# Split GELU times gate on one core: the steps in which the first tile is computed

## The chip, the cores and the metric

The kernel runs on one core of a Trainium2 chip. The core has engines that work side by side: ScalarE (ACT) computes functions element by element, VectorE (DVE) multiplies and adds tensors, SyncE (SP) issues transfers, and sixteen DMA engines move data between the chip's main memory (HBM) and the on-chip memory (SBUF, 128 partitions). TensorE and GpSimd have no work here. The metric is the device time of one execution in microseconds (us). Before the change it is 469.36 us, the median of three runs from 469.31 to 469.44.

## The reference

```python
batch, seq, dim = (32, 512, 2048)
x = np.random.randn(batch, seq, dim).astype(np.float32)

half_dim = x.shape[-1] // 2
x1, x2 = (x[..., :half_dim].copy(), x[..., half_dim:].copy())
gelu_x1 = 0.5 * x1 * (1 + erf(x1 / np.sqrt(2)))
return (gelu_x1 * x2).astype(np.float32)
```

The input has 16,384 rows of 2,048 numbers, 134.2 MB. The first half of a row goes through GELU and is multiplied with the second half. The output has rows of 1,024 numbers, 67.1 MB.

## The kernel before, in words

The rows are cut into 16 tiles of 1,024 rows. In a tile each of the 128 partitions holds R = 8 rows next to each other, so that one partition's part of a load is one piece of 64 KB of HBM, and its part of a store one piece of 32 KB. There are two input buffers (`x0`, `x1`) and two output buffers (`o0`, `o1`), and tile i uses the buffers i % 2: even tiles share one pair and odd tiles the other.

Loads are issued on SP's queue (`load`, L49), q1 in the profile. Tile 0 is loaded in two halves of four rows per partition, each with a semaphore of its own (`first[0]`, `first[1]`), tile 1 in one piece; all three are issued ahead of the loop. Stores (`store`, L56) are issued on ACT's queue, q10 in the profile, but for the last two tiles, whose stores go on SP's queue. Tile 0 and tile 15 are stored in two halves of four rows per partition, all others in one piece.

In the loop each tile is computed in steps, runs of its eight rows. Every step is one ACTIVATE on ACT (GELU of the first half of the rows, from the input buffer into the output buffer, L87) and one multiply on DVE (output buffer times the second half of the rows, in place, L95), which waits for its ACTIVATE through `gelu_done`. Tiles 1 to 14 have steps of five and three rows; tiles 0 and 15 have steps of two, two and four (`steps` at L79). Shapes in the profile name the elements of one partition: 2, 3, 4, 5 rows are 128x2048, 128x3072, 128x4096, 128x5120.

What sets the order of the work is written out by hand:

- Each engine's queue runs in program order. On ACT a store's issue stands between the ACTIVATEs and waits there for `mul_done`, the count of multiplies that are done; whatever ACT has to do next stands behind it.
- For tile 0, the ACTIVATE of row 0 waits for `first[0]` and that of row 4 for `first[1]` (L82). For later tiles the first ACTIVATE waits for `ready[k]`, which counts both the tile's load and the last store out of the same output buffer. So a tile starts when its load has landed and the store of the tile two before it has too.
- After tile i, SP waits until its multiplies are done and issues the load of tile i + 2 (`if i + 2 < n_tiles` at the end of the loop).
- A transfer's rows (128, one for each partition) are spread over the sixteen DMA engines, eight for each, and followed on each engine by a small end marker that raises the semaphore.

```python
steps = ((0, 2), (2, 4), (4, 8)) if pieces else ((0, 5), (5, 8))
...
if pieces and hi % 4 == 0:
    if last:
        store(nc.sync, i, slice(hi - 4, hi), tail_stored)
    else:
        store(nc.scalar, i, slice(hi - 4, hi), ready[k])
```

Of the kernel before, what the change touches and what calls it, by code (L numbers as in the profile page):

```python
# [1 line left out]

# [4 lines left out]

GELU = mybir.ActivationFunctionType.Gelu


@with_exitstack
def kernel(
    ctx: ExitStack,
    tc: tile.TileContext,
    x: bass.AP,
    out: bass.AP,
):
    nc = tc.nc
    P = nc.NUM_PARTITIONS

    x_flat = x.flatten_outer_dims()
    out_flat = out.flatten_outer_dims()
    n_rows, dim = x_flat.shape
    half = dim // 2

    R = 8
    x_t = x_flat.rearrange("(n p r) d -> n p r d", p=P, r=R)
    o_t = out_flat.rearrange("(n p r) d -> n p r d", p=P, r=R)
    n_tiles = x_t.shape[0]
    x_bufs = [nc.alloc_sbuf_tensor(f"x{k}_tile", [P, R, dim], x.dtype) for k in range(2)]  # L30
    o_bufs = [nc.alloc_sbuf_tensor(f"o{k}_tile", [P, R, half], out.dtype) for k in range(2)]

    first = [nc.alloc_semaphore(f"first{j}") for j in range(2)]
    ready = [nc.alloc_semaphore(f"ready{k}") for k in range(2)]
    gelu_done = nc.alloc_semaphore("gelu_done")
    mul_done = nc.alloc_semaphore("mul_done")
    tail_stored = nc.alloc_semaphore("tail_stored")
    opened = nc.alloc_semaphore("opened")  # L40
    scrap = nc.alloc_sbuf_tensor("scrap_tile", [8, 128], x.dtype)
    n = {sem.name: 0 for sem in [*first, *ready, gelu_done, mul_done, tail_stored, opened]}

    def counted(ins, sem, by):
        ins.then_inc(sem, by)
        n[sem.name] += by

    def load(i, rows, sem):
        ins = nc.sync.dma_start(out=x_bufs[i % 2][:, rows, :], in_=x_t[i][:, rows, :])  # L49
        counted(ins, sem, 16)  # L50
        return ins

    def store(queue, i, rows, sem):
        queue.wait_ge(mul_done, n[mul_done.name])
        counted(
            queue.dma_start(out=o_t[i][:, rows, :], in_=o_bufs[i % 2][:, rows, :]), sem, 16  # L56
        )

    opening = nc.scalar.dma_start(out=scrap[:, :], in_=x_t[0][:8, 0, :128])
    counted(opening, opened, 16)
    for ins in (
        opening,
        load(0, slice(0, 4), first[0]),
        load(0, slice(4, 8), first[1]),
        load(1, slice(0, 8), ready[1]),
    ):  # L70
        tc.no_tile_sem_insts.add(ins.ins.name)
    tc.close()
    tc.compile()  # L73

    for i in range(n_tiles):
        k = i % 2
        last = i == n_tiles - 1
        pieces = i == 0 or last
        steps = ((0, 2), (2, 4), (4, 8)) if pieces else ((0, 5), (5, 8))  # L79
        for lo, hi in steps:  # L80
            rows = slice(lo, hi)
            if i == 0 and lo % 4 == 0:  # L82
                nc.scalar.wait_ge(first[lo // 4], 16)
            elif lo == 0:
                nc.scalar.wait_ge(ready[k], n[ready[k].name])
            counted(
                nc.scalar.activation(  # L87
                    out=o_bufs[k][:, rows, :], in_=x_bufs[k][:, rows, :half], func=GELU
                ),
                gelu_done,  # L90
                1,
            )
            nc.vector.wait_ge(gelu_done, n[gelu_done.name])
            counted(
                nc.vector.tensor_mul(  # L95
                    out=o_bufs[k][:, rows, :],
                    in0=o_bufs[k][:, rows, :],
                    in1=x_bufs[k][:, rows, half:],
                ),
                mul_done,  # L100
# [7 lines that stand above are left out]
        if not pieces:  # L108
            if i == n_tiles - 2:
                store(nc.sync, i, slice(0, R), tail_stored)  # L110
            else:
                store(nc.scalar, i, slice(0, R), ready[k])
        if i + 2 < n_tiles:
            nc.sync.wait_ge(mul_done, n[mul_done.name])
            load(i + 2, slice(0, R), ready[k])


    nc.scalar.wait_ge(opened, 16)
    nc.scalar.drain()  # L119
    for sem in (*first, *ready, opened):  # L120
        nc.scalar.sem_clear(sem)
    nc.vector.drain()
    nc.vector.sem_clear(gelu_done)
    nc.sync.sem_clear(mul_done)
    nc.sync.wait_ge(tail_stored, n[tail_stored.name]).then_inc(
        tail_stored, -n[tail_stored.name]
    )


# [1 line left out]
_INS = ['x']  # L131
_OUTS = [((32, 512, 1024), 'float32')]


# [23 lines left out]
```

## Time and profile before

| What | Value |
|---|---|
| Median of three runs | 469.36 us |
| Profiled execution, span from first to last instruction | 467.8 us |
| Median less span | 1.56 us |
| ACT busy | 115.5 us, 25% |
| DVE busy | 140.5 us, 30% |
| Moved by the DMA engines | 201.34 MB, mean 430 GB/s |
| Queue q1 (loads, last stores) | 142.61 MB, 70.6% of the engines' time |
| Queue q10 (the other stores) | 58.73 MB, 29.1% of the engines' time |

The profile is of one execution. It gives its span, and no other time of its own; the median of the runs stands 1.56 us above the span. Single instructions of tile 0 and of the last tile have these means: an ACTIVATE of 128x2048 takes 1,901 ns and one of 128x4096 3,608 ns; a multiply of 128x2048 takes 2,288 ns and one of 128x4096 4,424 ns.

The profile shows busy times of the engines, a row that gives the share of time in which the DMA engines were busy in each of 40 slices (9 is 90% or more), the packets of each DMA queue, and a chain of waits: the work that ended last, followed back step by step to what released it. A DMA packet of a load or store is one partition's piece, and "to landing" counts from a transfer's issue until its last end marker.

### The profile page before, as it was taken

The page shows a single profiled execution, that of the slowest core. Times are in us where ns is not written, and L with a number is a line of the kernel's source. Part 1 is how long each engine was busy: PE and PEld are TensorE (multiplying, and loading weights), DVE is VectorE, ACT ScalarE, POOL GpSimd, SP SyncE. Part 2 cuts the span into 40 slices and gives each one's busy share as a digit, 9 for nine tenths or more (in the row PEclk, how much of TensorE's full clock was granted, in tenths as well). Part 3 has the DMA queues.
Part 4 walks back from the last instruction along what each step waited for, and adds up shares of the span by engine and source line. Part 5 has one row for each costly group of instructions (what it writes and reads, how often), then busy time and mean ns, then how long its engine had stood idle before and what let it go on. Part 6 is the DMA issues. An engine that isn't in the chain of part 4 may idle for free.

```text
span 467.8 us, 154 instructions
## 1 busy us (share of the span) xinstructions
DVE 140.5 (30%) x34; ACT 115.5 (25%) x35; POOL 0.2 (0%) x4
## 2 busy tenths in 40 slices
DVE  0330515207051060511606115060150702507043
ACT  1320606041060410604105050050501506014060
POOL 0000000000000000000000000000000000000000
DMA  8999999999999999999999999999999999999988
GB/s 359 448 448 448 398 406 496 403 403 448 459 437 403 440 412 493 403 403 448 487 409 403 445 406 493 403 403 448 493 403 403 448 426 471 403 426 426 493 384 379
DMA packets 5057, 201.34 MB, mean 430 GB/s; under 512 B 568, under 2 KB 576, under 8 KB 576
## 3 DMA queue, kind: packets, MB, share of 16 engines
q1 hardware_dynamic: 2880, 142.61, 70.6%
q10 hardware_dynamic: 2176, 58.73, 29.1%
q14 instruction: 1, 0.01, 0.0%
HBM read 134.22 MB, written 67.11 MB: 430 GB/s over the span
## 4 chain that ended last, share of the span: by engine, by line
DMA 76%; DVE 14%; ACT 8%; ACTq 0%; SPq 0%; issue 0%
DMA out_dram<-o_tile 66%; DVE o_tile L95 14%; DMA x_tile<-in_x_dram 10%; ACT o_tile L87 8%; ACTq L119 0%; SPq L49 0%
## 5 line engine op out<-in xcount | busy, mean ns | idle before, releaser
L95 DVE TENSOR_TENSOR o_tile<-o_tile,x_tile 128x5120 f32<-128x5120 f32 (+3 forms) x34 | 140.5, 4171 | 319.7 <-ACT o_tile L87 319.7
L87 ACT ACTIVATE o_tile<-x_tile 128x5120 f32<-128x5120 f32 (+3 forms) x34 | 114.3, 3407 | 337.3 <-DMA out_dram<-o_tile 301.8
L87 ACT ACT_TABLE_LOAD x1 | 1.3, 1283 | 2.9 <-PEq L73 2.9
L142 POOL MEMSET const-bfloat16-1.0<- 128x1 bf16 x1 | 0.1, 102 | 0.0
L142 POOL MEMSET const-uint8-127<- 128x1 uint8 x1 | 0.1, 101 | 0.0
L142 POOL MEMSET const-float32-0.0<- 128x1 f32 x1 | 0.1, 99 | 0.2 <-issue 0.2
L142 POOL MEMSET const-float32-1.0<- 128x1 f32 x1 | 0.1, 98 | 0.0
## 6 DMA issues: line engine op xcount, KB each, us to landing
out_dram<-o_tile ACTq DMA_DIRECT2D x13, 4096.0 KB, 44.7
x_tile<-in_x_dram SPq DMA_DIRECT2D x2, 4096.0 KB, 16.7
out_dram<-o_tile ACTq DMA_DIRECT2D x2, 2048.0 KB, 34.4
out_dram<-o_tile SPq DMA_DIRECT2D x1, 4096.0 KB, 25.2
out_dram<-o_tile SPq DMA_DIRECT2D x2, 2048.0 KB, 7.8
x_tile<-in_x_dram SPq DMA_DIRECT2D x15, 44.4
scrap_tile<-in_x_dram ACTq DMA_DIRECT2D x1, 4.0 KB
```

Source lines behind the costliest of these rows:

```text
L87: nc.scalar.activation(out=o_bufs[k][:, rows, :], in_=x_bufs[k][:, rows, :half], func=GELU),
L95: nc.vector.tensor_mul(out=o_bufs[k][:, rows, :], in0=o_bufs[k][:, rows, :], in1=x_bufs[k][:, rows, half:],),
L142: nc = _bacc.Bacc("TRN2", target_bir_lowering=False, num_devices=1)
```

## The change

Tile 0 is computed in two steps of four rows each, where it had steps of two, two and four. The loads of tile 0 (two halves) and its stores (two halves of four rows, issued after the multiplies of rows 3 and 7) are the same, and so is every other tile.

```diff
         pieces = i == 0 or last
-        steps = ((0, 2), (2, 4), (4, 8)) if pieces else ((0, 5), (5, 8))
+        if i == 0:
+            steps = ((0, 4), (4, 8))
+        else:
+            steps = ((0, 2), (2, 4), (4, 8)) if last else ((0, 5), (5, 8))
         for lo, hi in steps:
```

On ACT and on DVE two instructions of 128x2048 become one of 128x4096, so that each of the two engines has one instruction less. In the changed file the lines behind the edit stand three lower: L87 becomes L90 and L95 becomes L98.

## The prediction

> **What bounds the kernel now.** I read the page first: ACT is busy 25% and DVE 30% of the span, while the DMA line stands at 9 in nearly every slice.
>
> ```profile
> DVE 140.5 (30%) x34; ACT 115.5 (25%) x35; POOL 0.2 (0%) x4
> ...
> DMA  8999999999999999999999999999999999999988
> ...
> HBM read 134.22 MB, written 67.11 MB: 430 GB/s over the span
> ```
>
> So the sixteen DMA engines are the bound; DVE and ACT together could rest half the time. The size of one transfer unit comes next. A load or store of 128 partitions is 128 rows, 8 for each DMA engine. Tile 0's second load lands 9.68 us after the first (22.45 against 12.77), so a row of 32 KB takes 1.21 us, one of 64 KB (a whole load) 2.42, one of 16 KB (half a store) 0.61. A tile is then 8 x 2.42 + 8 x 1.21 = 29.04 us, and 16 tiles 464.6 us of the 467.8. The rest is 1.7 us before the first row, 0.45 after the last, and about 1 us of small gaps and stretched rows. Nothing that happens on ACT or DVE can save more than this 1 us; it can only add idle time on the DMA engines.
>
> The chain of waits (start, length, what) seems to say something else, and shows where an edit could still matter:
>
> ```profile
> 1.64 45.36 DMA x_tile<-in_x_dram
> 46.99 0.02 issue
> 47.02 4.48 ACT o_tile L87
> ...
> 60.31 40.07 DMA out_dram<-o_tile
> 100.38 0.02 issue
> 100.40 4.48 ACT o_tile L87
> ...
> 403.75 44.74 DMA out_dram<-o_tile
> 448.49 0.02 issue
> 448.51 1.91 ACT o_tile L87
> ```
>
> It runs through the odd tiles: 1, 3, ... 15, each 58.0 us after the last. While an odd tile is computed, the DMA engines work off an even tile's rows (2 x 29.04 = 58.1), so the 13 us of ACT and DVE in each round are covered. Tile 0 is not in this chain at all. It touches it only through the order in which its stores' rows stand among the loads' rows.
>
> **Tile 0, step by step.** The timeline of before (start, length, instruction) gives the start; the durations of a step of four rows are already in the trace, from tile 0's second half and the last tile:
>
> ```profile
> 12.79 3.71 ACT L87 ACTIVATE o_tile<-x_tile 128x2048 f32<-128x2048 f32 x2 [8.65 <-DMA x_tile<-in_x_dram]
> 14.73 4.49 DVE L95 TENSOR_TENSOR o_tile<-o_tile,x_tile 128x2048 f32<-128x2048 f32 x2 [14.73 <-ACT o_tile L87]
> 19.26 0.38 ACTq L56 DMA_DIRECT2D out_dram<-o_tile  x1
> 22.47 3.62 ACT L87 ACTIVATE o_tile<-x_tile 128x4096 f32<-128x4096 f32 x1 [5.97 <-DMA x_tile<-in_x_dram]
> 26.12 4.42 DVE L95 TENSOR_TENSOR o_tile<-o_tile,x_tile 128x4096 f32<-128x4096 f32 x1 [6.89 <-ACT o_tile L87]
> 30.58 0.36 ACTq L56 DMA_DIRECT2D out_dram<-o_tile  x1
> ```
>
> Removed: two ACTIVATEs and two multiplies of 2048 elements (3.71 and 4.49 us). Added: one of each of 4096 (3.62 and 4.42). Busy time falls by 0.1 us on each engine, worth nothing beside an idle engine. What moves is the overlap: DVE began at 14.73, after half of ACT's work; now it begins after all of it, at 12.79 + 3.62 + 0.03 = 16.44, and ends at 20.86. The first store of tile 0 (call it A) is issued at **20.90 instead of 19.26, 1.64 us later**. Behind it on ACT's queue stands the GELU of rows 4 to 8, which waits for its load until 22.45; A's issue is over at 20.90 + 0.38 = 21.28, so 1.17 us of cover are left. From 22.47 on tile 0 is as before: the second store (B) and the load of tile 2 are issued at 30.58 and 30.57, with tile 1's load far from done (46.99). No other instruction moves on SP, ACT or DVE by itself.
>
> **What 1.64 us do to A's rows.** This is the first thing that the trace of before does not show directly. The DMA view by stretches shows how the two queues (q1: loads, q10: stores) take turns on every engine:
>
> ```profile
> q1 hardware_dynamic: 32, 1.05, 99.0%
> ...
> q10 hardware_dynamic: 16, 0.26, 152.8%
> ...
> q1 hardware_dynamic: 16, 1.05, 93.6%
> ...
> q10 hardware_dynamic: 16, 0.26, 122.2%
> ```
>
> These are the packets that start in 21.6 to 24.3 us, 24.3 to 24.7, 24.7 to 27.3 and 27.3 to 27.8. In the first, sixteen load rows of 64 KB (and tile 0's sixteen end markers); then sixteen store rows, sixteen load rows, sixteen store rows: one row of each queue in turn. A, issued at 19.26, got no turn at 21.66 to 22.11, where tile 1's first row started, but the one after it, at 24.36. An engine with nothing before it was quicker: the first load, issued at 0.73, had all its first rows under way between 1.73 and 2.30, that is 1.00 to 1.57 us after the issue. So A could have run from 20.3 to 20.8 on, and yet the next row, 0.8 to 1.9 us later, was another's: the choice is made ahead, by at least about 1.3 us on each engine, perhaps when the row before it starts.
>
> After the change A is there at 21.9 to 22.5, and the turn at 24.1 to 24.7 is about 2.2 us away. If the choice is made over 2.2 us ahead (one row of 64 KB is 2.42 us), A misses this turn and its first row starts near 26.8; if it is made 1.3 to 2.2 us ahead, nothing changes at all. I take the miss, because a choice at the start of a row of 2.42 us fits both, and one engine of sixteen that misses is enough.
>
> [...]
>
> **What a missed turn costs.** The rows of A, then B, then every later store stand one load row further back. Tile 1 gains: the eighth row of A is no longer ahead of its end marker, so it starts 0.61 us earlier, at 46.4. From tile 2 on each tile waits for the store before last in its output buffer, whose end now stands behind the next load's first row: starts move by 2.42 us (71.40 to 73.8, 100.40 to 102.8, and so on). That is no idle time: loads and stores are issued some 14 us before the queues ahead of them are empty (load 4 at 84.69, load 3 done at about 99), so the engines never starve, and the lag does not grow.
>
> It shows at the end. Behind store 13 stands no load any more but store 14 on q1, a row of 1.21 us: tile 15 starts at 448.51 + 1.21 = 449.72, and its last store is issued 1.21 us later. In before:
>
> ```profile
> 454.97 5.57 SPq L56 DMA_DIRECT2D out_dram<-o_tile  x2
> 455.76 4.42 DVE L95 TENSOR_TENSOR o_tile<-o_tile,x_tile 128x4096 f32<-128x4096 f32 x1 [0.81 <-ACT o_tile L87]
> ```
>
> The second of these issues starts at 454.97 + 5.57 - 0.33 = 460.21 and its rows from 462.07 on, without a gap behind the store before it. So 1.86 us lie between them, and an issue needs 1.00 to 1.57 (the first load, above): 0.29 to 0.86 us of cover. The loss is 1.21 less this: **0.35 to 0.92 us**, middle 0.64. The store before it (454.97, first row at 457.2) has 2.23 us between, and its loss of at most 0.55 lies inside the later one.
>
> [...]
>
> **The sum.** Span 467.8 + 0.64 = 468.4; the median of the runs, 469.36, lies 1.56 us above the profiled span, which I keep: **470.0 us**. About 0.2%, or 0.94 us, is what a measurement of this kernel can tell from no change, so the forecast itself is "no change", a little on the slow side.
>
> **The rivals.**
> 1. No missed turn: A takes its row at 24.36 as before. Everything after it stands where it stood: 469.36. For it: the lead that before proves is only 1.3 us. Against it: a choice at row starts explains before as well.
> 2. Slower: a missed turn with nothing to hide it at the end. If an issue from SP needs all of the 1.86 us, the whole 1.21 is lost: 470.57; and if the engines run dry they start again with a stretched row, as the first did (1.64 to 2.06 instead of 1.21: 0.43 to 0.85 more), up to 471.4. It decides from an issue-to-row time above 1.59 us (1.21 - 0.94 = 0.27 of cover left). For it: before needs A to be not yet chosen 1.2 to 1.6 us after its issue. Against: no row shows such a time on an engine that was free.
> 3. Faster: the chain of waits taken at its word. Tile 1 starts 0.61 us earlier and all odd tiles with it, 468.75. Against it: the bytes. 464.6 us of rows leave about 1 us in the whole span to save, and stores that come late push odd tiles too. Even so it ends 0.61 below, inside no-change; a gain over 0.94 would need nearly all gaps gone.
>
> **Chances.** Forecast (miss, partly covered) 0.52; no miss 0.25; miss with no cover 0.20; faster 0.03. Faster by over 0.2%: 0.03, allowing rival 3 more than its sum; slower by over 0.2%: 0.20; within: 0.77. The range runs from just under 469.36 (469.2) into rival 2 (470.9); it leaves out the 0.03 below and the upper half of rival 2.
>
> **What the changed profile would show.** Tile 0: one ACTIVATE of 128x4096 at 12.8, a multiply at 16.4 to 20.9, the store's issue at 20.9; if that is not so, the first step is wrong. A's first row near 26.8 (a stretch 24.3 to 24.7 without q10 packets) and A landing near 49.1 mean the miss; q10 packets at 24.36 and a landing near 47.2 mean rival 1. Starts of tiles 1, 2, 3 and 15 at 46.4, 73.8, 102.8 and 449.7 show the lag carried through; 47.0, 71.4, 100.4 and 448.5 that it was not. The last store's issue at 461.4 with first rows near 462.7 shows the loss at the end; rows of 64 KB at another pace than 2.42 us would make all of it wrong.

## The result, and the profile after

The changed kernel takes 480.20 us (median of four runs, 479.76 to 482.09) against 469.39 us before (median of four runs taken beside it; 469.36 was the figure of three runs ahead of the prediction): a ratio of 1.0239, 95% interval 1.0220 to 1.0258. It is 10.8 us slower, where 470.0 with a range of 469.2 to 470.9 was predicted. The profiled execution has a span of 478.5 us, 10.7 more than before.

The page of the changed kernel, the lines that answer to those of before:

```profile
DVE 140.4 (29%) x33; ACT 115.4 (24%) x34; POOL 0.2 (0%) x4
...
DMA  8999999999999999999999999999999999999998
...
HBM read 134.22 MB, written 67.11 MB: 421 GB/s over the span
```

ACT and DVE do the same work within 0.1 us, and the DMA engines still have no idle slice. They move the same bytes, but at 421 GB/s instead of 430. So the 10.7 us are not idle time: the DMA engines are busy throughout and do less in it.

Its timeline of tile 0 (start, length, instruction):

```profile
12.76 3.62 ACT L90 ACTIVATE o_tile<-x_tile 128x4096 f32<-128x4096 f32 x1 [8.63 <-DMA x_tile<-in_x_dram]
16.41 4.42 DVE L98 TENSOR_TENSOR o_tile<-o_tile,x_tile 128x4096 f32<-128x4096 f32 x1 [16.41 <-ACT o_tile L90]
20.86 0.38 ACTq L56 DMA_DIRECT2D out_dram<-o_tile  x1
22.47 3.62 ACT L90 ACTIVATE o_tile<-x_tile 128x4096 f32<-128x4096 f32 x1 [6.09 <-DMA x_tile<-in_x_dram]
```

This step is as predicted: the first store (A) is issued at 20.86, 1.60 us later than before, and the GELU of the second half still starts at 22.47.

The DMA view of the changed kernel in two time windows, 24.3 to 24.75 us (two queues) and 26.6 to 27.3; the columns are packets, MB, share of 16 engines:

```profile
q1 hardware_dynamic: 3, 0.20, 114.6%
q10 hardware_dynamic: 8, 0.13, 67.9%
...
q10 hardware_dynamic: 8, 0.13, 43.6%
```

Before, sixteen store rows stood in the first window. Now eight do, and the other eight engines start A's first row a load row later, from 26.9 us on. Half of the engines caught the turn and half missed it.

The chain of waits of the changed kernel at the places shown of before:

```profile
1.63 45.91 DMA x_tile<-in_x_dram
47.53 0.02 issue
47.56 4.48 ACT o_tile L90
...
60.85 42.17 DMA out_dram<-o_tile
103.02 0.02 issue
103.05 4.48 ACT o_tile L90
...
413.70 45.59 DMA out_dram<-o_tile
459.28 0.02 issue
459.31 1.91 ACT o_tile L90
```

Up to tile 3 the lag is the predicted one (102.8 forecast, 103.05 seen). From there it grows: tile 15 starts at 459.31, 10.80 us after its start of before, where 1.21 was forecast. A round of two tiles takes 59.4 us ((459.31 - 103.05) / 6), where before took 58.0. The busy times in windows of 58 us say the same; the last column is GB/s, first two lines of before, then two of the changed kernel:

```profile
108.00:166.00 58.00, 17.53 (x5) 14.24 (x4) 0.00 (x0) 1.00 1.00 434
340.00:398.00 58.00, 17.47 (x5) 14.25 (x4) 0.00 (x0) 1.00 1.00 434
```

```profile
108.00:166.00 58.00, 17.07 (x4) 12.78 (x4) 0.00 (x0) 1.00 1.01 426
340.00:398.00 58.00, 17.52 (x4) 14.25 (x4) 0.00 (x0) 1.00 1.01 425
```

Where in a tile the time goes is seen in the DMA view of the changed kernel in 221 to 222 us, as the second row of load 8 starts on eight engines, and in 225.5 to 226, as the third does:

```profile
q1 hardware_dynamic: 8, 0.52, 161.2%
...
q1 hardware_dynamic: 8, 0.52, 241.8%
```

161.2% of sixteen engines for 1 us, spread over 8 rows, is 3.22 us a row; 241.8% for 0.5 us is 2.42. So on these eight engines the second row of 64 KB was stretched by a third, and the third was not. Taken over all packets of the changed kernel, what rows of 64 KB take beyond their usual length (2.4175 us, in the mean of the sixteen engines; called the stretch below) costs 0.61 to 0.88 us in every load from 4 to 15 (load i is that of tile i), nearly all of it on the second and third row, together 9.1 us; in loads 2 and 3 almost nothing (0.04 and 0.02). Before, no load after load 1 has more than 0.04. Load 1 adds 0.4 (0.80 against 0.38). The remaining 1.2 us was not traced further; it is of the size of the later end that the prediction described.

The eight engines that caught the turn are stretched as much as the eight that missed it. They come to the second row of load 8 two microseconds later, in 223 to 224.3 us, and seven of them show there:

```profile
q1 hardware_dynamic: 7, 0.46, 104.9%
```

104.9% of sixteen engines for 1.3 us, spread over 7 rows, is 3.12 us a row, on engines whose own rows stand in the order of before. Over loads 4 to 15 the two halves lose 8.9 and 9.0 us an engine. So what a missed turn did here was not confined to the engine that missed.

### The profile page after: what moved, and what is told of

Read it like the earlier page. It is cut to its first block, busy times and chain, and to the rows that moved or that the text cites. A ratio compares the mean times of both kernels' runs of the same rounds, so it can differ in the third digit from the quotient of the medians.

```text
span 478.5 us, 152 instructions
## 1 busy us (share of the span) xinstructions
DVE 140.4 (29%) x33; ACT 115.4 (24%) x34; POOL 0.2 (0%) x4
## 4 chain that ended last, share of the span: by engine, by line
DMA 76%; DVE 14%; ACT 8%; ACTq 0%; SPq 0%; issue 0%
DMA out_dram<-o_tile 67%; DVE o_tile L98 14%; DMA x_tile<-in_x_dram 10%; ACT o_tile L90 8%; ACTq L122 0%; SPq L49 0%
## 5 line engine op out<-in xcount | busy, mean ns | idle before, releaser
L98 DVE TENSOR_TENSOR o_tile<-o_tile,x_tile 128x5120 f32<-128x5120 f32 (+3 forms) x33 | 140.4, 4292 | 330.6 <-ACT o_tile L90 330.6
L90 ACT ACTIVATE o_tile<-x_tile 128x5120 f32<-128x5120 f32 (+3 forms) x33 | 114.2, 3505 | 348.2 <-DMA out_dram<-o_tile 312.0
```

What stands on the lines that cost most here:

```text
L90: nc.scalar.activation(out=o_bufs[k][:, rows, :], in_=x_bufs[k][:, rows, :half], func=GELU),
L98: nc.vector.tensor_mul(out=o_bufs[k][:, rows, :], in0=o_bufs[k][:, rows, :], in1=x_bufs[k][:, rows, half:],),
```

## The experiments

Three theories were open at first. **Turn theory**: what matters is whether an engine's turn comes before or after A is there. **Lateness theory**: each microsecond that A is late costs alike. **Step theory**: the larger instructions themselves cost it.

### When does the first store get its turn?

An extra GELU was put on ACT between tile 0's first GELU and the store, into the output buffer of tile 1, which is idle then.

```diff
+            if i == 0 and hi == 4:
+                nc.scalar.activation(out=o_bufs[1][:, 0:4, :], in_=x_bufs[0][:, 0:4, :half], func=GELU)
+                nc.scalar.activation(out=o_bufs[1][:, 4, 0:640], in_=x_bufs[0][:, 0, 0:640], func=GELU)
             if pieces and hi % 4 == 0:
```

(Here as in e2, with the old steps; e1 has the first of the two alone; e4 has the changed steps, and two rows in place of the 640 elements. There is no run of an e3, the changed steps with the store meant for 21.3 us; e7 takes its place.)

> Tile 0 in the old steps of two, two and four rows; ACT computes an extra GELU into the idle output buffer o1 so that the first store is issued near 20.1 us instead of 19.26. Turn theory: a queue's first row gets its turn about 3.5 us after the issue (all sixteen engines took it at 24.36 to 24.68 from 19.26, eight of sixteen at 24.39 to 24.67 from 20.86), so 20.1 is early enough for all sixteen; they stay in step and the time is 469.4, within 0.3. Lateness theory (every microsecond that the store is later costs about the same, 10.8 us for 1.6): about 475. Step theory (the larger instructions cost it): 469.4.

> Old steps again, with a longer extra GELU, so that the store is issued near 20.9 us as in the changed kernel. Turn theory: some engines catch the turn at 24.4 and some miss it; load rows are stretched at the start of every tile, and the time is 477 to 483. Lateness theory: 480. Step theory: 469.4.

> The same with an extra GELU of six rows, store issued near 21.9 us. Turn theory: again all miss together, 469.7 to 470.3, the same as at 21.3. Lateness theory: about 487. Step theory: 480.

Measured: e1 469.33 us, e2 469.37, e4 480.76 (before on the same chip 469.34). These edits did not hold the store back as they were meant to. The timeline of e2:

```profile
14.70 4.49 DVE L95 TENSOR_TENSOR o_tile<-o_tile,x_tile 128x2048 f32<-128x2048 f32 x2 [14.70 <-ACT o_tile L87]
16.37 3.60 ACT L104 ACTIVATE o_tile<-x_tile 128x4096 f32<-128x4096 f32 x1
19.22 0.38 ACTq L56 DMA_DIRECT2D out_dram<-o_tile  x1
19.88 0.72 ACT L105 ACTIVATE o_tile<-x_tile 128x640 f32<-128x640 f32 x1
```

The store behind the GELU on ACT's queue is issued at 19.22, while that GELU still runs (until 16.37 + 3.60 = 19.97). It came right behind the end of the multiply that it waits for (14.70 + 4.49 = 19.19), and did not wait for the computation ahead of it. So e1 and e2 only repeat the kernel before, and e4 the changed one (store at 20.93, five engines of sixteen catch the turn). They do show that extra work on ACT there cost nothing.

In the next four the store waits for the extra GELU through a semaphore.

```diff
+                nc.scalar.activation(...).then_inc(held, 1)
+                nc.scalar.wait_ge(held, 1)
             if pieces and hi % 4 == 0:
```

> Old steps of two, two and four rows in tile 0; the first store now really waits, on a semaphore, for an extra GELU of four rows into the idle output buffer, and should be issued near 20.1 us. Turn theory: a first row gets its turn about 3.5 us after the issue (sixteen of sixteen engines at 24.36 to 24.68 from 19.26, eight at 24.39 to 24.67 from 20.86, five at 24.43 to 24.80 from 20.93), so from 20.1 all sixteen catch it: 469.4, within 0.3. Lateness theory (each microsecond of lateness costs alike, 10.8 us for 1.6): about 475. Step theory (the larger instructions cost it): 469.4.

> Old steps, the first store held back by the extra GELU to near 20.9 us, where the changed kernel has it. Turn theory: some engines catch the turn at 24.4 and some miss it; load rows are stretched at the start of each tile from the fourth load on; 477 to 483. Lateness theory: 480. Step theory: 469.4.

> The changed kernel (steps of four and four), the first store held back to near 21.3 us. Turn theory: 21.3 + 3.5 lies behind the last engine's turn (24.7), so all sixteen miss it together, stay in step, and pay the missed turn alone: 469.7 to 470.3. Lateness theory: about 483. Step theory: 480.

> The changed kernel, the first store held back to near 21.9 us. Turn theory: all sixteen miss together as at 21.3, 469.7 to 470.3. Lateness theory: about 487. Step theory: 480.

| Kernel | A issued | engines that caught the turn near 24.5 | time, us |
|---|---|---|---|
| e5, old steps | 20.18 | 16 | 469.34 |
| e6, old steps | 20.66 | 15 in the profile | 470.73 (469.20 to 483.29) |
| changed kernel | 20.86 | 8 | 480.20 |
| e4, changed steps | 20.93 | 5 | 480.76 |
| e7, changed steps | 21.15 | 0 | 477.66 (477.06 to 482.15) |
| e8, changed steps | 21.78 | 0 | 478.01 |

(Before on the same chip as e5 to e8: 469.28.) The step theory falls, since e6 with the old steps reaches 483 us in some of its runs. The lateness theory falls, since e5 is 0.9 us late and free, and e8 0.6 us later than e7 at the same time. The first half of the turn theory, that A's issue decides which engines catch the turn, stands. But its 3.5 us from the issue to the end of the running row does not: the one engine of e6 that missed ended its row 4.01 us after the issue, while engines of the changed kernel caught the turn at 3.53. The start of that row sorts the engines better (the trace does not name a packet's engine; a packet is put on the engine whose row before it ended where it starts). In the before kernel, e4 to e9, e12 and the changed one, every engine whose row started 1.20 us or more after A's issue took A next, every one whose row started 0.98 us or less after it took another load row, and between the two both occur; e6's engine that missed has 0.97, its lowest. The second half falls. e7 and e8 missed on all sixteen engines, as the prediction had it, and were expected at 470.0; they took 8 us more. The same views as above, of e7 (no packet starts in 24.75 to 26.6 us; this is 26.6 to 27.3):

```profile
q10 hardware_dynamic: 16, 0.26, 87.3%
```

```profile
224.00:282.00 58.00, 17.52 (x4) 12.78 (x5) 0.00 (x0) 1.00 0.99 423
340.00:398.00 58.00, 17.52 (x4) 14.25 (x4) 0.00 (x0) 1.00 1.01 428
```

All sixteen are in step with one another, and yet move 423 to 428 GB/s from 224 us on: rows of loads 4 to 15 are stretched by 0.21 to 0.73 us a load, together 6.1. So a new question: what stretches them?

### Is it computing, or certain addresses?

e9 leaves out nearly all computation of tiles 2 to 14 of the changed kernel (the multiply is cut like the GELU shown):

```diff
+            cut = half if i < 2 or last else 8
...
-                    out=o_bufs[k][:, rows, :], in_=x_bufs[k][:, rows, :half], func=GELU
+                    out=o_bufs[k][:, rows, :cut], in_=x_bufs[k][:, rows, :cut], func=GELU
```

e12 moves the source of the loads:

```diff
+    x_off = x_flat[4 : 4 + (n_tiles - 1) * R * P].rearrange("(n p r) d -> n p r d", p=P, r=R)
...
+        src = x_off if 0 < i < n_tiles - 1 else x_t
```

> The changed kernel with nearly all computation of tiles 2 to 14 left out: their ACTIVATEs and multiplies treat 8 elements of each row instead of 1,024, so the output of these tiles is mostly not computed; all transfers stay. Question: are the load rows at the start of each tile stretched (2.42 to about 3.2 us) because ACT and DVE use the on-chip memory at that time? Compute theory: no stretch left, 469.5 to 470.5. Order theory (the stretch comes from the transfers' own order after the missed turn): still stretched, 476 to 482.

> The changed kernel with the loads of tiles 1 to 14 taken four input rows (32 KB) further on in HBM, so these tiles' results are those of other rows; same sizes, same order. If the stretch comes from certain HBM addresses that loads and stores touch at the same time, it moves to other rows of the load or its size changes: anything from 470 to 490. If it is a matter of order and timing alone: the same stretch on the second and third row, 478 to 482.

Measured: e9 480.13 us, e12 480.62 (before 469.28). The stretch of e9's loads 4 to 15 comes to 5.8 us, that of e12 to 7.4, on rows 2 to 4. In e9 one engine caught the turn and fifteen missed it, so its 5.8 stand beside e7's 6.1 and not beside the 9.1 of eight and eight. Its time is longer than this mean says, since one engine lags: load 14 ends there at 428.59 us, on the other fifteen by 424.24. A line of e9 in a window of 58 us:

```profile
340.00:398.00 58.00, 0.33 (x3) 0.35 (x2) 0.00 (x0) 1.00 1.01 428
```

DVE and ACT are busy for 0.33 and 0.35 us of 58, and the rate is as low as in e7. So the computing is not needed for the stretch. That it is not a matter of addresses is shown for this one shift of 32 KB only.

### Is it the order of the rows?

Read packet by packet on one engine (put together as above), around the start of load 4 (x4.1 is the first row of load 4, S1.8 the last row of tile 1's store, x3! and S1! the end markers):

```
before   x3.8  S1.8  x3!   S1!   x4.1  S2.1  x4.2  S2.2
e7       x3.8  S1.7  x3!   S1.8  x4.1  S1!   x4.2  S2.1
```

In these orders an end marker takes a turn of its own, as a row does (a spare row and its marker shifted the order by two turns in e10 and e11, below). The kernel before starts 32 packets of q1 in 21.64 to 22.2 us, the sixteen first rows of load 1 and sixteen of under 512 B, tile 0's markers:

```profile
DMA packets 32, 1.05 MB, mean 1873 GB/s; under 512 B 16, under 2 KB 16, under 8 KB 16
```

So in e7, one turn behind, two store rows stand back to back and right behind them two load rows. Before, loads and stores alternate. If that is the cause, the queues can be put straight by a transfer that does nothing but take turns:

```diff
+    def spare_row():
+        ins = nc.sync.dma_start(out=spare[:, :], in_=x_t[0][:16, 0, :128])
+        counted(ins, opened, 16)
+        return ins
...
         load(1, slice(0, 8), ready[1]),
+        spare_row(),
```

e10 is e7 with it, e11 the kernel before with it, e16 the changed kernel with it. e13 is the kernel before with such a transfer on ACT's queue behind A instead; e17 has both, the one on ACT's queue with 32 rows.

> The changed kernel with the first store held back to 21.2 us (477.7 us before), and one spare transfer of 16 small rows on SP's queue between the loads of tile 1 and tile 2. The spare row and its end marker take two turns of q1, so the stores, one turn behind the loads after the miss, come out one turn ahead: no two load rows and no two store rows stand next to each other at a tile's start any more. Order theory: stretch gone, 469.4 to 470.3. Lateness theory (a late first store itself costs): 477.7 as without it.

> The kernel before with the same spare row: nothing is late, and the stores come out two turns ahead of the loads, so that two store rows stand next to each other at a tile's start. Order theory: any order with two rows of a kind in a row costs, 472 to 480. If only stores that lag behind cost: 469.4 to 470. Lateness theory: 469.4.

> The kernel before, with one spare transfer of 16 small rows on ACT's queue right behind the first store. Nothing is late, no instruction of the work moves; the spare row and its end marker take two turns of q10, so the stores come out two turns behind the loads. Lag theory (stores one or more turns behind the loads, load rows back to back at each tile's start, are what stretches the rows): 476 to 482, rows of 64 KB over 2.6 us on the second to fourth row of loads 4 to 15. If only the lateness of the first store or engines out of step cost: 469.4 plus a later end (tile 15 starts two rows of 1.21 us later, of which 0.3 to 0.9 is covered), 471.0 to 471.6, without stretch.

> The changed kernel as it is (first store at 20.9 us, some engines catch their turn and some miss it), with the spare row and marker on SP's queue between the loads of tiles 1 and 2. It puts the engines that missed one turn ahead and the others two turns ahead; neither order was stretched alone (469.56 and 469.59). If the order one turn behind is the cause: 469.4 to 470.5. If engines out of step with one another are the cause: still 476 to 482.

> The kernel before with nothing late, a spare transfer of one row per engine on SP's queue (two turns with its marker) and one of two rows per engine on ACT's queue behind the first store (three turns): the stores come out exactly one turn behind the loads on all sixteen engines, as in the kernel that was held to 21.2 us (477.7). If being one turn behind is the cause, whatever brought it about: 476 to 480, rows 2 and 3 of loads 4 to 15 stretched. Two turns behind gave 471.1 without stretch. If only a late first store or engines out of step cost: 469.7 to 470.5.

| Kernel | stores against loads | order around load 4 | stretch of loads 4 to 15, us | time (before beside it) |
|---|---|---|---|---|
| before | in step | as above | under 0.1 | 469.39 |
| e10 | one turn ahead | S1.8 x3.8 S1! x3! S2.1 x4.1 S2.2 | 0.0 | 469.56 (469.28) |
| e11 | two ahead | x3.7 S1! x3.8 S2.1 x3! S2.2 x4.1 | 0.0 | 469.59 (469.28) |
| e13 | two behind | S1.6 x3! S1.7 x4.1 S1.8 x4.2 S1! x4.3 | 0.0 | 471.11 (469.26) |
| e17 | one behind | as e7 | 5.7 | 477.35 (469.30) |
| e7 | one behind | as above | 6.1 | 477.66 (469.28) |
| e16 | one or two ahead | both, by engine | 0.0 | 471.54 (469.30) |

e10 and e17 settle it. e10 has A as late as e7 and is as fast as before; e17 has A where before has it, its rows caught by all sixteen engines at 24.5 to 25.0, and is as slow as e7. One line of each in a window of 58 us, e10 first:

```profile
340.00:398.00 58.00, 17.52 (x5) 14.25 (x4) 0.00 (x0) 1.00 1.00 434
```

```profile
340.00:398.00 58.00, 17.52 (x4) 14.24 (x4) 0.00 (x0) 1.00 1.00 424
```

The expectations that any row pair of one kind costs (e11) and that stores behind by any number of turns do (e13) were wrong: e11 has load pairs and store pairs too, and e13 load pairs at every tile (x4.2, x4.3), at 434 GB/s:

```profile
340.00:398.00 58.00, 17.52 (x4) 14.24 (x5) 0.00 (x0) 1.00 1.00 434
```

What was slow was being exactly one turn behind (e7 and e17, 6.1 and 5.7 us of stretch), where the pair of loads follows the pair of stores directly. e13's 1.85 us is of the size of the later end: two rows of 1.21 less the 0.29 to 0.86 of cover that the prediction worked out give 1.56 to 2.13. It is not the end alone: its loads 1 and 2 are stretched by 0.99 us (0.42 before), and tile 15 starts 2.84 us later (451.35), not 2.42. In e16 engines out of step did not stretch rows by themselves, once none was one turn behind (0.0 us in loads 4 to 15); it ends 2.2 us late, 1.0 of it in loads 1 and 2 (1.44 against 0.42 us of stretch), the rest was not traced.

### Which of the row pairs is needed?

```diff
-                store(nc.scalar, i, slice(0, R), ready[k])
+                store(nc.scalar, i, slice(0, 4), ready[k])
```

```diff
-            load(i + 2, slice(0, R), ready[k])
+            load(i + 2, slice(0, 4 if i + 3 < n_tiles else R), ready[k])
```

> The changed kernel with the first store held to 21.2 us (477.7 us, all engines one turn behind, stretched from the fourth load on), with the stores of tiles 1 to 13 cut to their first four rows per partition (16 KB pieces): half of those tiles' output is left out. In the held kernel loads 2 and 3, behind stores of 16 KB, were not stretched, load 4 and later, behind stores of 32 KB, were. If the long store rows (two of 1.21 us back to back) are needed for the stretch: no load is stretched, about 406 us (63 us less transfer than 469.4). If two load rows back to back are enough: stretched by 0.3 us or more a load, 410 to 414.

> The same held kernel, whole stores, but the loads of tiles 2 to 14 cut to their first four rows per partition (32 KB pieces); the other rows of these tiles are computed from older data. If two long load rows back to back (4.84 us of loading alone) are needed: no stretch, about 343 us (126 us less transfer). If the back-to-back store rows of 32 KB alone are enough: load rows of 1.21 us stretched by a fifth or more at the start of each tile, 347 to 352.

e14 (the first edit, in e7) took 407.08 us, and its packets show the order of e7 at every tile without any stretch (0.00 us in loads 2 to 15). So behind stores of 16 KB a row, pairs of long load rows cost nothing here; this fits loads 2 and 3 of e7, which were free and stand behind tile 0's store rows of 16 KB. e15 took 349.42 (347.25 and 351.59) and answers nothing: with loads so short SP's queue ran empty near 61 us, and when it was filled again loads and stores alternated as in before.

## Why the prediction was wrong

- **The steps on ACT and DVE, and A's issue**: right. 16.44, 20.86 and 20.90 were forecast for the multiply's start and end and the issue; 16.41, 20.83 and 20.86 were seen, and nothing behind A on ACT's queue moved.
- **A misses its turn**: right in kind, and so was its reason, a choice at the start of the row that runs (above). Eight engines missed, eight did not. "One engine of sixteen that misses is enough" treated this as one case; e6 shows that the number matters (470.3 us in the profiled execution with one engine behind, 483.29 at most).
- **What a missed turn does to the order**: right. Tiles 2 and 3 were forecast at 73.8 and 102.8; the changed kernel has 74.01 and 103.05, e7 74.15 and 103.21. Tile 1 was forecast 0.61 us earlier; it came 0.54 later. Eight engines still had all of A's rows to pass, so nothing was gained there, and load 1's rows were stretched by 0.80; in e7, where all sixteen missed, it came at 47.00, as before (47.02), with 0.91 of stretch.
- **"That is no idle time ... and the lag does not grow"**: this is the step that failed. The engines never starved, as argued, but the sum took a row of 64 KB as 2.42 us in any order. With half of the engines in the order one turn behind it is not, on any of the sixteen: 0.61 to 0.88 us a load, twelve loads, 9.1 of the 10.7 us. The prediction did name "rows of 64 KB at another pace" as what would undo it, but gave that no chance.
- **The end**: not contradicted, and not seen alone. e13, two turns behind without stretch from load 3 on, loses 1.85 us, within what the cover of the last store leaves (1.56 to 2.13), but part of its lag comes from loads 1 and 2.
- **The chances**: 0.20 stood for slower, through a rival (no cover at the end, 470.6 to 471.4) that was not the cause. No case had the order itself as a price. Before had shown one order only, in which nothing changed for 400 us, and a cost of another order was bounded at nothing without a row that showed it.

Shown by these runs: A's issue time decided which engines missed their turn (none of sixteen at 20.18 us, eight at 20.86, all at 21.15); a miss left those engines' stores one turn behind; that order, brought about by a late store (e7) or with nothing late (e17), stretched load rows at the start of loads 4 to 15 (6.1 and 5.7 us together), and with eight engines in it the rows of the other eight too (8.9 and 9.0); a spare row that ended it gave the time back (e10, 469.56 us). With one engine behind (e6's profile) that engine lost 0.8 us in twelve loads and the others nothing. Not shown: why a pair of 32 KB store rows followed by a pair of 64 KB load rows slowed the loads, and nearly only their second to fourth rows; and how this reached engines that are not behind. It happened with nearly no computing (e9, 5.8 us), one shift of addresses did not end it (e12, 7.4), and shorter store rows did (e14, 0.00). Why the changed kernel, with eight engines behind, loses more (9.1 us) than e7 with all sixteen (6.1) stays open too.

## What to carry to other kernels

In this kernel, which the DMA engines bound, two queues took turns row by row (before, a load row of 2.42 us and a store row of 1.21), and which was ahead was set once, by the moment at which the emptier queue was first filled (A issued at 20.18 us: caught by all sixteen engines; at 21.15: by none); it lasted as long as neither queue ran empty (in e15 one did near 61 us, and the order changed). A change that moved one early store by 1.6 us flipped it for the rest of the run. In a kernel of this kind, read the order of packets on the queues before and after, and price the new order as an unknown when the trace shows only the old one. Here a spare transfer of one small row per engine, with its end marker, shifted the order by two turns (from in step to two ahead in e11, from one behind to one ahead in e10) and tested this in one run.

## What the runs showed of the hardware that was not expected

- On a busy engine A's first row came after the row that was running, and whether it did was settled about when that row started: rows that started 0.98 us or less after A's issue were followed by another load row, rows that started 1.20 us or more after it by A. That is near the 1.00 to 1.57 us from issue to first row on engines that were free.
- From load 3 on, rows of 64 KB took 2.42 us in every order that was run but one (engines each lost under 0.02 us a load); in that one, stores of 32 KB a turn behind, the second row of load 8 took 3.22 us in the changed kernel, and on its other eight engines 3.12 (above).
- In e7 the stretch hit engines unequally and drove them apart: the first rows of load 4 lie within 0.36 us on its sixteen engines, those of load 15 within 3.6.
- A transfer's issue on ACT's queue did not wait for the end of the ACTIVATE ahead of it: 19.22 us against 19.97 in e2.
